# A two-block model on one core: four of six convolution filter blocks made beside the first output product, first loads reordered, and a scheduler that knows matmul kinds

## The chip, the cores and the metric

The kernel runs on one core of a Trainium2 chip. The number that counts is the device time of one launch in microseconds (us); lower is better. The core has five engines that run their own instruction streams and wait for one another by semaphores: TensorE (PE, with its weight loads shown apart as PEld), VectorE (DVE), ScalarE (ACT), GpSimd (POOL) and SyncE (SP), which here only issues DMA transfers.

## The reference

The program takes 512 tokens of width 1024 and a context of 256 tokens through a first model of two blocks, and its result through a second model of two layers with an MLP each. Everything is float32. Of the first model this matters here:

```python
for i in range(DEPTH):
    shift, scale, gate = modulation(c, w_mod[i], b_mod[i])        # silu(c) @ w_mod + b_mod
    h = rmsnorm(x, norm_g[i]) * (1 + scale) + shift
    if i == 0:                                                    # "L0"
        cshift, cscale, _ = modulation(c_ctx, w_mod[i], b_mod[i])
        hc = rmsnorm(ctx, norm_g[i]) * (1 + cscale) + cshift
        a_val, a_gate, q, k, v, b_gate = split(h @ ev_w_in)
        ck, cv = split(hc @ ev_w_in[:, k and v columns])
        # six rotary attention heads over context + tokens, a pooling mixer, gates, then
        x = x + gate * (y @ ev_w_out)                             # "L0out"
    else:                                                         # "L1"
        k = hyena_filters(...)      # from constants and small weights alone, not from x
        z = gate_o * (fft_long_conv(z, k[:, o]) + skip[o] * z)    # for o = 0, 1
        x = x + gate * (y @ od_w_out)
```

The long-convolution filters `k` are needed only in L1, but depend on nothing that comes earlier.

## The kernel before

Every product of two float32 matrices is done as three matmuls of split operands: a high part (rounded to the type fp32r) and a low part (what is left), high x high, high x low, low x high. Splitting a page costs one ScalarE activation (high) and one VectorE subtract (low). Activations, filters and tables lie in `NPG` = 52 pages of 128 x 512 floats (`pg`); weights come through a ring of three 512 KB slots (`raw`) and are split into `wh` pages. All of SyncE's transfers stand in one queue in a fixed order.

The body of the program does not run instructions; it records them into a `Plan` (from line 152 on). `Plan.schedule` then plays all engines against a model of costs (`model`, about line 250) and latencies, and puts each engine's instructions in an order: a candidate's priority is when its result is due on TensorE, shifted by `bias[phase]`, with windows `wins[(pool, phase)]` that bound how far ahead a phase may take pages or PSUM banks. `emit` (line 558) then issues all of them, which is why every row of the profile has line L558. Work that has no place of its own in the program text, such as an attention head, is a generator in the list `chains`, and `step()`, called between two gemm pieces, lets it record its next piece; `drain_chains()` (line 1589) records what is left.

The phases at the program's head, in the order in which they are recorded, and with the names that later rows use:

1. Phase "": constants, the vectors `vec` (biases, norms and the conditioning vectors), x into `xT`, the context into four pages `cT`.
2. `filt0`: two small layers that give the hidden values `hst` of the filter network.
3. `m0` (line 1232): the modulation of block 0. The activated conditioning vectors `cc` (two columns: token and context) are multiplied with `w0`, 1024 x 2048 in 16 slots of 512 KB, each with two unsplit float32 matmuls of 512 columns; small transposes against `ident` bring the rows back to columns, and a VectorE copy writes them (`m`, twice 128 x 16). From them come the scales `sc` and shifts `sh`.
4. `filt` (lines 1280 to 1352): six filter blocks, three column blocks `cb` by two orders `o`. A block loads its part of `hy_w3`, makes four 128 x 512 pages `h` by matmuls, multiplies by a decay table, sums absolute values into `acc` (the norm `hyn`), splits `h`, multiplies by the split transform matrices `cst_filt`, forms the even and odd parts `ke`, `ko`, and writes them to the DRAM tensor `kf`. The pieces are recorded by `filters()`.
5. `L0norm` (line 1369): norm sums and the scaled, shifted and split activations of context and x (`SCALAR_TENSOR_TENSOR` with `sc`, then with `sh`), the rotary table `rope` in four pages.
6. `L0kv`, `L0q`, `L0 gemm 0..2`, heads 0 to 5, then `L0out` (line 1600), the L1 norm and the L1 products, in which the hyena chains read `kf`.

A further background, phase `mods`, sums the modulation weights of all later layers with 128 VectorE instructions of their own (`mraw`).

## Time and profile before

| | |
|---|---|
| median of 3 runs | 1899.92 us (1899.1 to 1905.7) |
| the profiled execution's own time | 1898.62 us |
| its span in the trace | 1896.8 us |
| TensorE busy | 1834.3 us, 97% of the span |
| VectorE busy | 1542.9 us, 81% |
| ScalarE busy | 1026.6 us, 54% |
| GpSimd busy | 196.8 us, 10% |
| mean granted TensorE clock | 0.982 |

The own time is 1.8 us longer than the span, and the median lies 1.3 us above the own time. "Busy" counts the time in which an engine executes; TensorE's includes matmuls that run slower than they could. The granted clock is the share of full TensorE speed that the chip gave.

### The profile page before, as it was taken

The page shows a single profiled execution, that of the slowest core. Times are in us where ns is not written, and L with a number is a line of the kernel's source. Part 1 is how long each engine was busy: PE and PEld are TensorE (multiplying, and loading weights), DVE is VectorE, ACT ScalarE, POOL GpSimd, SP SyncE. Part 2 cuts the span into 40 slices and gives each one's busy share as a digit, 9 for nine tenths or more (in the row PEclk, how much of TensorE's full clock was granted, in tenths as well). Part 3 has the DMA queues.
Part 4 walks back from the last instruction along what each step waited for, and adds up shares of the span by engine and source line. Part 5 has one row for each costly group of instructions (what it writes and reads, how often), then busy time and mean ns, then how long its engine had stood idle before and what let it go on. Part 6 is the DMA issues. An engine that isn't in the chain of part 4 may idle for free.

```text
span 1896.8 us, 33344 instructions
## 1 busy us (share of the span) xinstructions
PE 1834.3 (97%) x12451; PEld 1645.8 (87%) x12451; DVE 1542.9 (81%) x3419; ACT 1026.6 (54%) x2112; POOL 196.8 (10%) x206
## 2 busy tenths in 40 slices
PE   7999999999999999999999999989999999999997
PEld 2789887988888988868888899988877889999997
DVE  6877898789986799677999877698966899776677
ACT  5666666453334565654664445574754457444455
POOL 0230010001110010021200000032101220000000
PEclk9899999999999999999999999999999989999999
DMA  8743543355432356311247422334541124323321
GB/s 281 221 132 103 193 154 112 122 194 177 137 133 78 119 169 210 96 45 45 90 161 240 155 100 89 102 108 167 184 145 45 46 78 140 106 90 101 100 90 68
DMA packets 88244, 243.19 MB, mean 128 GB/s; under 512 B 10060, under 2 KB 27248, under 8 KB 87825
## 3 DMA queue, kind: packets, MB, share of 16 engines
q1 hardware_dynamic: 88080, 241.05, 38.7%
q8 instruction: 98, 1.61, 0.3%
q14 instruction: 66, 0.53, 0.1%
HBM read 232.63 MB, written 8.39 MB: 127 GB/s over the span
## 4 chain that ended last, share of the span: by engine, by line
PE 83%; DVE 12%; ACT 2%; issue 2%; DMA 1%; POOL 0%; SPq 0%; DVEq 0%; ACTq 0%
PE ps L558 83%; DVE pg L558 7%; DVE sa L558 2%; ACT pg L558 2%; DVE wh L558 1%; DVE mraw L558 1%; ACT wh L558 0%; DMA raw<-in_w_dram 0%; DVE w L558 0%; POOL xT L558 0%; DMA vec<-in_vec_dram 0%; DVE xT L558 0%; SPq L558 0%; DVE sb L558 0%; ACT L558 0%
## 5 line engine op out<-in xcount | busy, mean ns | idle before, releaser
L558 PE MATMUL ps<-pg,wh 128*128 128x256 f32 (+1 forms) x6336 | 1101.6, 329 | 4.2 <-ACT pg L558 3.8
L558 PEld LDWEIGHTS ps<-pg,wh 128*128 128x128 f32 x6336 | 921.0, 190 | 107.5 <-ACT pg L558 5.7
L558 PE MATMUL ps<-wh,pg 128*128 128x256 f32 (+2 forms) x2976 | 379.6, 283 | 5.3 <-ACT pg L558 4.7
L558 ACT ACTIVATE wh<-raw 128x1024 fp32r<-128x1024 f32 (+3 forms) x280 | 257.8, 924 | 226.6 <-PE ps L558 222.6
L558 PEld LDWEIGHTS ps<-wh,pg 128*128 128x128 f32 x2976 | 364.3, 189 | 9.8 <-ACT pg L558 6.1
L558 DVE TENSOR_TENSOR pg<-pg 128x256 f32<-128x256 f32 (+4 forms) x656 | 317.5, 516 | 45.4 <-ACT pg L558 35.7
L558 DVE TENSOR_TENSOR wh<-raw,wh 128x1024 fp32r<-128x1024 f32 (+3 forms) x280 | 295.4, 1060 | 69.0 <-ACT wh L558 52.7
L558 ACT ACTIVATE pg<-pg 128x256 f32<-128x256 f32 (+5 forms) x630 | 274.0, 472 | 143.3 <-DVE pg L558 81.1
L558 PE MATMUL ps<-pg 128*128 128x256 f32 (+9 forms) x1776 | 264.6, 303 | 9.5 <-DVE pg L558 3.6
L558 PEld LDWEIGHTS ps<-pg 128*128 128x128 f32 (+5 forms) x1776 | 225.6, 188 | 43.5 <-issue 16.5
L558 DVE TENSOR_TENSOR pg<-pg,ps 128x256 f32<-128x256 f32 (+1 forms) x392 | 174.8, 465 | 59.6 <-PE ps L558 55.7
L558 POOL TENSOR_TENSOR pg<-pg 128x512 f32<-128x512 f32 (+4 forms) x101 | 120.7, 1202 | 858.0 <-ACT pg L558 434.6
L558 DVE TENSOR_TENSOR pg<-ps,pg 128x512 fp32r<-128x512 f32 (+8 forms) x278 | 146.4, 561 | 42.1 <-ACT pg L558 27.3
L558 DVE CUSTOM_DVE_ANT_0 mraw<-mraw,crow 128x1024 f32<-128x1024 f32 x128 | 155.4, 1220 | 8.5 <-DMA mraw<-in_wmT_dram 5.5
L558 ACT ACTIVATE pg<-ps 128x512 fp32r<-128x512 f32 (+4 forms) x212 | 105.0, 523 | 100.1 <-PE ps L558 80.0
L558 ACT COPY pg<-ps 128x256 f32<-128x256 f32 (+4 forms) x192 | 82.7, 445 | 106.2 <-PE ps L558 87.5
L558 ACT ACTIVATE wh<-w 128x512 fp32r<-128x512 f32 x112 | 70.1, 629 | 124.1 <-PE ps L558 104.4
L558 DVE TENSOR_TENSOR wh<-w,wh 128x512 fp32r<-128x512 f32 x112 | 76.7, 686 | 29.1 <-PE ps L558 17.2
L558 PE MATMUL ps<-ident,pg 128*128 128x128 f32 (+1 forms) x513 | 83.9, 279 | 5.0 <-DVE pg L558 3.8
L558 PEld LDWEIGHTS ps<-ident,pg 128*128 128x128 f32 (+1 forms) x513 | 63.3, 144 | 16.2 <-ACT pg L558 4.2
L558 ACT ACTIVATE pg<-ps,sa 128x512 f32<-128x512 f32 (+3 forms) x112 | 60.5, 550 | 29.6 <-DVE sa L558 19.1
L558 DVE TENSOR_REDUCE sa<-ps 128x1 f32<-128x512 f32 (+4 forms) x96 | 51.2, 571 | 11.4 <-PE ps L558 11.1
(139 smaller groups left out, 1095.4 us busy)
## 6 DMA issues: line engine op xcount, KB each, us to landing
mraw<-in_wmT_dram SPq DMA_DIRECT2D x128, 512.0 KB, 4.3
raw<-in_w_up_dram SPq DMA_DIRECT2D x64, 512.0 KB, 3.3
raw<-in_w_down_dram SPq DMA_DIRECT2D x64, 512.0 KB, 3.3
raw<-in_w_in_dram SPq DMA_DIRECT2D x32, 512.0 KB, 4.1
raw<-in_od_w_in_dram SPq DMA_DIRECT2D x28, 512.0 KB, 3.6
raw<-in_ev_w_in_dram SPq DMA_DIRECT2D x20, 512.0 KB, 3.7
raw<-in_w_dram SPq DMA_DIRECT2D x16, 512.0 KB, 4.1
raw<-in_w_o_dram SPq DMA_DIRECT2D x16, 512.0 KB, 3.3
```

The source lines that it names most:

```text
L558: o.fn(*[r(v) for v in o.args], **{k: r(v) for k, v in o.kw.items()})
```

## The change

1. `NF = 2`: only the first two filter blocks are recorded in the start (`filt`). The other four become a chain `filt 1`, appended after `drain_chains()` and stepped by the pieces of L0out and, through a new `step()` in `cross()`, by those that lead from L0out over the L1 norm into the first L1 product. The chain loads and splits the transform matrices a second time; for the split pages three of the four pairs lie in the weight pool `w4`.
2. A block's work is recorded in two parities, with a yield after each page. The odd part `ko` is a VectorE subtract from PSUM (before: a ScalarE copy and a GpSimd subtract), the norm is finished block by block, the decay table is loaded per block and parity.
3. `w0` comes in 32 loads of 256 KB into `pg` pages instead of 16 of 512 KB into the `raw` ring. The loads of x, context and `vec` are phases of their own, with biases of their own for SyncE (`("SP", "m0"): -30`).
4. The rotary table is stored once per head pair and broadcast: 0.5 MB instead of 1 MB, two pages instead of four, twice as many VectorE products of half the size.
5. The scheduler's model charges TensorE for a change between four kinds of matmul (`TURN`: fp32r, transpose, float32, small float32), prefers to stay in a kind (`stick`), and many biases and windows have other values.

The program has 12,059 TensorE matmuls before and after. VectorE has 3453 instructions instead of 3419, ScalarE 1911 instead of 1919, GpSimd 204 instead of 206, SyncE 588 transfers instead of 564.

```diff
--- before.py
+++ after.py
-FL = (0,)
...
-KO = (1,1,)
+NF = 2
...
-    fill=0.5, ahead=3.0, near=0.0,
+    fill=0.5, ahead=2.0, near=0.0, stick=10,
...
-        "": -15, "L0 gemm 0": -8, "L0 gemm 2": -8, "L0norm": 20, "L0out": -215, "L0q": 106, "L1 gemm 0": 145,
...
+        "": -15, ("SP", "L1out"): 8, ("SP", "m0"): -30, "L0 gemm 0": -8, "L0 gemm 2": -8, "L0norm": 20,
+        "L0out": -15, "L0q": 106, "L1 gemm 0": 265, "L1 gemm 1": 22, "L1f": 68, "L1norm": 270, "L1out": -7,
...
+    TURN = ((0.0, 0.0, 0.085, 0.185), (0.0, 0.0, 0.09, 0.12), (0.085, 0.0, 0.0, 0.1), (0.3, 0.2, 0.21, 0.0))
+    stick = 10.0
...
+                op.kind = 0 if f else 3 if a[1].shape[0] <= 64 or w in (31, 64) else 2
...
+                    if s <= ms + self.near:
+                        v = o.bl + (self.stick if e == "PE" and o.kind == kind > 1 else 0.0)
+                        if v > bb:
+                            b, bb, bs = o, v, s
...
+                s, kind = max(s, tfree[e] + self.TURN[kind][o.kind]), o.kind
...
             pl.ph = ph
             for f in fs:
                 f()
+                step()
...
+    pl.ph = "x"
     for k in range(0, KT, 4):
         D_(xall[:, k:k + 4], a["xT"][:, k:k + 4])
     cT = [pg(name="cT") for _ in range(KT // 2)]
+    pl.ph = "ctx"
     for k in range(KT // 2):
         D_(cT[k], a["ctxT"][:, k])
+    pl.ph = "vec"
...
     for j in range(2):
         pa = [mmt(), mmt()]
         for k in range(KT):
-            raw = wraw()[:, :D]
-            D_(raw, a["w0"][j, k])
             for hh in range(2):
-                T.matmul(pa[hh][0:2], cc[:, k, :], raw[:, hh * S:(hh + 1) * S], start=(k == 0), stop=(k == KT - 1))
-        row = w4()
+                raw = pg()
+                D_(raw, a["w0"][j, k, :, hh * S:(hh + 1) * S])
+                T.matmul(pa[hh][0:2], cc[:, k, :], raw, start=(k == 0), stop=(k == KT - 1))
+        row = [pg(), pg()]
         for hh in range(2):
...
-    def hyena_filters(hst):
+    def hyena_filters(hst, todo):
         fm = []
         for i in range(4):
             fr = pg()
             D_(fr, a["cst_filt"][:, i * S:(i + 1) * S])
-            fm.append(split(fr))
+            t = [pl.alloc("w4", S).bitcast(F32R) for _ in range(2)] if i < 3 else [None, None]
+            fm.append(split(fr, hi=t[0], lo=t[1]))
         yield
-        for cb in range(3):
-            dec = [pg(), pg()]
-            for i in range(2):
-                D_(dec[i].rearrange("p (t n) -> p t n", t=2),
-                                  a["cst_decay"].rearrange("p (t n) -> p t n", t=4)[:, 2 * i:2 * i + 2, cb * 256:cb * 256 + 256])
-            for o in range(2):
...
-                acc = None
+        for cb, o in todo:
+            w3 = pg()
...
+            acc, xs = None, []
+            for par in range(2):
+                dec = pg()
+                D_(dec.rearrange("p (t n) -> p t n", t=2),
+                   a["cst_decay"].rearrange("p (t n) -> p t n", t=4)[:, 2 * par:2 * par + 2, cb * 256:cb * 256 + 256])
                 ab = []
-                for jt in range(4):
+                for jt in (2 * par, 2 * par + 1):
                     ps = axt()
                     js = slice(jt * P, jt * P + P)
                     for d_ in range(2):
...
                     h = pg()
-                    dj = dec[jt // 2][:, (jt % 2) * 256:(jt % 2) * 256 + 256]
+                    dj = dec[:, (jt % 2) * 256:(jt % 2) * 256 + 256]
                     V.tensor_mul(h.rearrange("p (d n) -> p d n", d=2), ps.rearrange("p (d n) -> p d n", d=2),
                                  dj.unsqueeze(1).to_broadcast([P, 2, 256]))
                     hb, ha = pg(), hp()
...
                         V.tensor_copy(h[0:1, 256:], h[0:1, :256])
                     else:
                         G.tensor_tensor(acc, acc, ha, op=OP.add)
-                    ab.append(split(h, eng=V if jt in FL else G))
-                ps = axt()
-                for i in range(2):
-                    T.matmul(ps[:, i:i + 1], acc[:, i * P:(i + 1) * P], ones[:, 0:1], start=True, stop=True)
-                V.tensor_copy(hyn[:, o, 2 * cb:2 * cb + 2], ps[:, :2])
+                    ab.append(split(h))
+                    yield
+                if par:
+                    ps = axt()
+                    for i in range(2):
+                        T.matmul(ps[:, i:i + 1], acc[:, i * P:(i + 1) * P], ones[:, 0:1], start=True, stop=True)
+                    hy = hyn[:, o, 2 * cb:2 * cb + 2]
+                    V.tensor_scalar(hy, ps[:, :2], 1e-6, 1024.0, op0=OP.add, op1=OP.mult)
+                    V.reciprocal(hy, hy)
                 for ft in range(2):
...
-                    xs, ke, ko = pg(), pg(), pg()
-                    A.copy(xs, px)
-                    V.tensor_add(ke, xs, py)
-                    if KO[ft]:
-                        ys = pg()
-                        A.copy(ys, py)
-                        G.tensor_tensor(ko, xs, ys, op=OP.subtract)
-                    else:
-                        V.tensor_sub(ko, xs, py)
+                    ps = axt()
+                    for rs in range(2):
+                        fh, fl = fm[2 * par + rs]
+                        cs = slice(rs * 256, rs * 256 + 256)
+                        for i in range(2):
+                            fs = slice(i * 256 + ft * P, i * 256 + ft * P + P)
+                            xh, xl = ab[i]
+                            mm3(ps[:, cs], (fh[:, fs], fl[:, fs]), (xh[:, cs], xl[:, cs]), i == 0, i == 1)
+                    if not par:
+                        xs.append(pg())
+                        A.copy(xs[ft], ps)
+                        continue
+                    ke, ko = pg(), pg()
+                    V.tensor_add(ke, xs[ft], ps)
+                    V.tensor_sub(ko, xs[ft], ps)
...
                 yield
-        V.tensor_scalar(hyn.rearrange("p a b -> p (a b)"), hyn.rearrange("p a b -> p (a b)"), 1e-6, 1024.0,
-                        op0=OP.add, op1=OP.mult)
-        V.reciprocal(hyn.rearrange("p a b -> p (a b)"), hyn.rearrange("p a b -> p (a b)"))
-        yield
-
...
-    filters(9)
+
+    todo = [(cb, o) for cb in range(3) for o in range(2)]
+    for _ in hyena_filters(hst, todo[:NF]):
+        pass
...
-    rope = [pg(name="rope") for _ in range(4)]
-    for i in range(4):
+    rope = [pg(name="rope") for _ in range(2)]
+    for i in range(2):
...
     q_block(0)
-    filters()
...
     drain_chains()
+    chains.append(("filt 1", hyena_filters(hst, todo[NF:])))
```

The table of numbers acts through the order of the instructions. Three places show it; every instruction of the kernel is issued at one line, L558 before and L564 after.

SyncE, the queue's head (`in_w` is w0, `in_hy_w` the filter network's weights, `in_cst_filt` the transform matrices). Before:

```order
L558 DMA pg<-in_cst_emb_dram 33x512
L558 DMA pg<-in_hy_w_dram 33x64
L558 DMA raw_368<-in_w_dram 128x1024
L558 DMA raw_369<-in_w_dram 128x1024
L558 DMA pg<-in_hy_w_dram 64x64 x2
L558 DMA raw_370<-in_w_dram 128x1024
L558 DMA vec_366<-in_vec_dram 128x83
L558 DMA pg<-in_hy_w_dram 64x2x256 x2
L558 DMA pg<-in_cst_decay_dram 128x2x256 x2
L558 DMA ident<-in_cst_ident_dram 128x128
L558 DMA pg<-in_cst_filt_dram 128x512 x4
L558 DMA pg<-in_hy_w_dram 64x2x256 x4
```

After:

```order
L564 DMA pg<-in_cst_emb_dram 33x512
L564 DMA pg<-in_hy_w_dram 33x64
L564 DMA vec_366<-in_vec_dram 128x83
L564 DMA pg<-in_hy_w_dram 64x64 x2
L564 DMA pg<-in_hy_w_dram 64x2x256 x2
L564 DMA pg<-in_cst_decay_dram 128x2x256
L564 DMA pg<-in_cst_filt_dram 128x512
L564 DMA ident<-in_cst_ident_dram 128x128
L564 DMA pg<-in_cst_filt_dram 128x512
L564 DMA pg<-in_w_dram 128x512 x2
L564 DMA pg<-in_ctxT_dram 128x512
L564 DMA pg<-in_cst_decay_dram 128x2x256
```

The `vec` load moves from eighth to third transfer and the context comes early; the first piece of w0 moves from third to twelfth place, after filter weights, a decay table and two transform matrices. The last piece of w0 stands behind 16.54 MB in the new queue, behind 15.75 MB in the old.

VectorE, from the second modulation copy `m_397` on. Before:

```order
L558 COPY m_397<-ps 128x16
L558 TENSOR_TENSOR pg<-pg,ps 128x512
L558 TENSOR_TENSOR pg<-pg 128x256 x3
L558 TENSOR_TENSOR pg<-pg 128x512
L558 TENSOR_TENSOR pg<-pg 128x256 x7
L558 TENSOR_TENSOR pg<-ps,pg 128x512 x2
L558 COPY hyn<-ps 128x2
L558 TENSOR_TENSOR pg<-ps,pg 128x512
L558 TENSOR_TENSOR pg<-pg,ps 128x512
L558 TENSOR_TENSOR pg<-ps,pg 128x512
L558 TENSOR_TENSOR pg<-pg 128x256 x2
```

After:

```order
L564 COPY m_397<-ps 128x16
L564 TENSOR_TENSOR wh_376<-raw_370,wh_375 128x1024
L564 TENSOR_TENSOR sc_399<-m_397,vec_366 128x8 x2
L564 SCALAR_TENSOR_TENSOR sc_399<-sc_399,vec_366 128x8 x2
L564 SCALAR_TENSOR_TENSOR pg<-pg,sc_399,ps 128x256 x4
L564 SCALAR_TENSOR_TENSOR pg<-pg,sh_398 128x256
L564 SCALAR_TENSOR_TENSOR pg<-xT,sc_399,ps 128x512
```

Before, filter pages (`pg<-ps,pg`, `pg<-pg`, `hyn`) follow the copy, and `sc` comes 24 rows after the last of these; after, `sc` and the first scaled activations (`xT` is the token input) follow almost at once, and no filter instruction stands between.

TensorE, in L0out from the last block of 17 matmuls of head 5 on (`wh` are split weights of L0out, `w_2940`, `w_2953`, `w_3002` transform matrices). Before:

```order
L558 MATMUL ps<-pg 128x256 x17
L558 MATMUL ps<-pg,wh_375 128x512
L558 MATMUL ps<-pg,wh_376 128x512
L558 MATMUL ps<-pg,wh_375 128x512 x2
L558 MATMUL ps<-pg,wh_376 128x512
L558 MATMUL ps<-pg,wh_375 128x512 x2
L558 MATMUL ps<-pg,wh_376 128x512
L558 MATMUL ps<-pg,wh_373 128x512 x2
```

After:

```order
L564 MATMUL ps<-pg 128x256 x17
L564 MATMUL ps<-pg,wh_371 128x512 x2
L564 MATMUL ps<-pg,wh_372 128x512
L564 MATMUL ps<-pg,w_2940 128x256
L564 MATMUL ps<-pg,wh_373 128x512
L564 MATMUL ps<-pg,w_2940 128x256
L564 MATMUL ps<-pg,w_2953 128x256
L564 MATMUL ps<-pg,wh_373 128x512
L564 MATMUL ps<-pg,w_2940 128x256 x2
L564 MATMUL ps<-pg,wh_374 128x512
L564 MATMUL ps<-pg,w_2953 128x256
L564 MATMUL ps<-pg,w_2940 128x256
```

Before, L0out's matmuls stand in runs of their own; after, matmuls of 256 columns of the moved filter blocks lie between them one by one. The same 256 filter matmuls that stood ahead of or among the first projections now lie in heads 4 and 5, L0out, the L1 norm and the first two L1 products. From about matmul 9210 of 12,059 to the end the orders of TensorE are the same, also from 5432 to 7427.

## Rows read from the trace of the kernel before

**Rows 1.** the page, its span and section 1 (busy us, share of span, instructions).
```profile
span 1896.8 us, 33344 instructions
PE 1834.3 (97%) x12451; PEld 1645.8 (87%) x12451; DVE 1542.9 (81%) x3419; ACT 1026.6 (54%) x2112; POOL 196.8 (10%) x206
```

**Rows 2.** the chain that ended last: by engine, then one long piece.
```profile
PE 83%; DVE 12%; ACT 2%; issue 2%; DMA 1%; POOL 0%; SPq 0%; DVEq 0%; ACTq 0%
...
117.99 117.18 PE ps L558 x808
```

**Rows 3.** windows: engines' busy us (instructions), granted PE clock, DMA share, GB/s.
```profile
0.00:20.00 20.00, 9.64 (x20) 1.62 (x20) 9.35 (x22) 5.76 (x11) 1.56 (x10) 1.00 0.89 271
20.00:60.00 40.00, 39.15 (x166) 17.79 (x167) 31.75 (x72) 24.03 (x48) 2.72 (x3) 0.96 0.78 266
60.00:100.00 40.00, 34.55 (x240) 31.46 (x241) 36.36 (x86) 28.20 (x55) 16.64 (x14) 0.87 0.78 230
100.00:120.00 20.00, 17.32 (x143) 16.91 (x143) 19.75 (x44) 16.69 (x38) 9.34 (x8) 1.00 0.24 68
120.00:235.00 115.00, 115.00 (x795) 105.73 (x794) 89.30 (x215) 68.64 (x159) 1.72 (x2) 1.00 0.45 147
235.00:330.00 95.00, 89.59 (x538) 76.98 (x537) 84.43 (x200) 60.11 (x140) 4.83 (x3) 0.96 0.43 139
330.00:600.00 270.00, 270.00 (x1712) 243.02 (x1711) 227.80 (x424) 108.54 (x173) 29.41 (x23) 1.00 0.44 148
```

**Rows 4.** PE's timeline to 137.6 us: start, length, form, count, idle before.
```profile
9.27 6.14 PE L558 MATMUL ps<-raw,cc 128*2 128x512 f32 x8 [5.21 <-ACT cc L558]
32.18 1.88 PE L558 MATMUL ps<-raw,cc 128*2 128x512 f32 x4
67.19 0.41 PE L558 MATMUL ps<-ident,w 2*128 2x2 f32 x4
98.23 1.76 PE L558 MATMUL ps<-wh,pg 128*128 128x256 f32 x13
117.99 1.70 PE L558 MATMUL ps<-pg 128*128 128x256 f32 x12 [2.49 <-DVE pg L558]
...
119.53 18.07 PE L558 MATMUL ps<-wh,pg 128*128 128x256 f32 x152
```

**Rows 5.** DVE's timeline from the second modulation copy on.
```profile
67.91 0.16 DVE L558 COPY m<-ps 128x16 f32<-128x16 f32 x1
...
87.28 0.16 DVE L558 TENSOR_TENSOR sc<-m,vec 128x8 f32<-128x8 f32 x1
...
90.22 2.43 DVE L558 SCALAR_TENSOR_TENSOR pg<-pg,sc,ps 128x256 f32<-128x256 f32 x6
...
112.59 5.35 DVE L558 SCALAR_TENSOR_TENSOR pg<-xT,sc,ps 128x512 f32<-128x512 f32 x8
```

**Rows 6.** VectorE's groups by form: count, busy us, mean ns, idle before and releasers.
```profile
L558 DVE TENSOR_TENSOR pg<-pg 128x256 f32<-128x256 f32 x250 | 100.5, 428 | 12.6 <-ACT pg L558 9.7 <-DMA pg<-in_hy_w_dram 1.6 <-POOL pg L558 0.6
L558 DVE TENSOR_TENSOR pg<-pg 128x512 fp32r<-128x512 f32 x116 | 77.8, 688 | 11.9 <-ACT pg L558 6.5 <-PE ps L558 4.8
L558 DVE TENSOR_TENSOR pg<-pg,ps 128x512 f32<-128x512 f32 x76 | 50.9, 680 | 14.8 <-PE ps L558 14.3 <-ACT pg L558 0.2
L558 DVE TENSOR_TENSOR pg<-ps,pg 128x512 f32<-128x512 f32 x78 | 50.3, 680 | 9.7 <-PE ps L558 9.4
```

**Rows 7.** windows again: the first loads, then heads and first output product.
```profile
5.00:30.00 25.00, 17.67 (x46) 4.62 (x47) 14.85 (x33) 8.45 (x19) 0.87 (x1) 0.93 1.02 317
30.00:65.00 35.00, 35.00 (x168) 17.83 (x167) 28.91 (x65) 22.41 (x45) 2.72 (x3) 1.00 0.69 239
380.00:460.00 80.00, 80.00 (x470) 70.22 (x469) 74.17 (x129) 34.19 (x49) 7.05 (x5) 1.00 0.56 192
460.00:520.00 60.00, 60.00 (x385) 54.16 (x384) 58.57 (x120) 19.33 (x30) 10.29 (x8) 1.00 0.42 139
```

**Rows 8.** what SyncE's DMA queue waited for, 0 to 120 us: total, times, longest.
```profile
SPq L558 <- PE ps L558: 28.6, 15, 4.4
```

More of the change, by code (lines that the diff above doesn't have):

```diff
@@ L137 @@
     __slots__ = ("eng", "fn", "args", "kw", "deps", "succ", "cost", "bufs", "idx", "bl", "npred", "est", "tab",
-                 "bytes", "cols", "start", "fin", "due", "ph", "ret", "ss", "se", "port", "other", "est2")
+                 "bytes", "cols", "start", "fin", "due", "ph", "ret", "ss", "se", "port", "other", "est2", "kind")
 class Eng:
@@ L257, in model @@
             if m == "transpose":
-                op.cost, op.cols = 0.109, 256 * a[1].shape[0] / P
+                op.cost, op.cols, op.kind = 0.109, 256 * a[1].shape[0] / P, 1
             else:
@@ L474, in schedule @@
                 for s, o in cand:
-                    if s <= ms + self.near and o.bl > bb:
-                        b, bb, bs = o, o.bl, s
+                    if s <= ms + self.near:
+                        v = o.bl + (self.stick if e == "PE" and o.kind == kind > 1 else 0.0)
+                        if v > bb:
+                            b, bb, bs = o, v, s
                 if bs < ps:
@@ L778, in tile_two_blocks @@
         D_(t, a[n])
+    pl.ph = ""
     def vcol(name):
@@ L1352, in hyena_filters @@
                 yield
-        V.tensor_scalar(hyn.rearrange("p a b -> p (a b)"), hyn.rearrange("p a b -> p (a b)"), 1e-6, 1024.0,
-                        op0=OP.add, op1=OP.mult)
-        V.reciprocal(hyn.rearrange("p a b -> p (a b)"), hyn.rearrange("p a b -> p (a b)"))
-        yield
-    filt = hyena_filters(hst)
-    def filters(n=99):
-        old, pl.ph = pl.ph, "filt"
-        for _ in range(n):
-            if next(filt, filt) is filt:
-                break
-        pl.ph = old
-    filters(9)
+    todo = [(cb, o) for cb in range(3) for o in range(2)]
+    for _ in hyena_filters(hst, todo[:NF]):
+        pass
     pl.ph = "L0norm"
@@ L1399, in ropeit @@
             t1, t2 = pg(), pg()
[L1400 to L1405 removed]
+            for tt in range(2):
+                ts = slice(tt * 256, tt * 256 + 256)
+                rs = slice((2 * tp + tt) * P, (2 * tp + tt) * P + P)
+                G.tensor_tensor(t1[:, ts].rearrange("p (h f) -> p h f", h=2), q[:, ts].rearrange("p (h f) -> p h f", h=2),
+                                rope[0][:, rs].unsqueeze(1).to_broadcast([P, 2, P]), op=OP.mult)
+                qv = q[:, ts].rearrange("p (h a s f) -> p h a s f", h=2, s=2, f=32)
+                sv = rope[1][:, rs].rearrange("p (a s f) -> p a s f", s=2, f=32)
+                tv = t2[:, ts].rearrange("p (h a s f) -> p h a s f", h=2, s=2, f=32)
+                for s in range(2):
+                    V.tensor_mul(tv[:, :, :, s], qv[:, :, :, 1 - s], sv[:, :, s].unsqueeze(1).to_broadcast([P, 2, 2, 32]))
             V.tensor_add(q, t1, t2)
```

53 lines of the change are left out of this document (18 added, 35 removed), and 32 rows, old and new, of the table wins.

## The prediction

> **What bounds the kernel now.** I began with the page's first section. TensorE is busy for 97% of a span of 1896.8 us, VectorE for 81% [rows 1]: nothing but TensorE's work and the holes in it sets the time. The chain of waits says the same, 83% TensorE and 12% VectorE, and its piece from 117.99 to 235.17 us has no hole [rows 2]. Since the matmuls stay the same in number and form, the change can only win holes, stretches at a lower clock and turns between kinds of matmul, or make new ones.
>
> So I next looked at windows, to find the holes [rows 3]. TensorE idles 10.36 us in the first 20, 0.85 in 20 to 60, 5.45 in 60 to 100 and 2.68 in 100 to 120: 19.3 us in 120. From 120 to 235 it is never idle, from 330 to 600 never either. Its clock is granted at 0.96 in 20 to 60 and at 0.87 in 60 to 100. If only the levels 1.2 and 2.4 GHz alternate, a mean of 0.87 is 40 x 0.13 = 5.2 us lost, and 0.96 another 1.6: 6.8 us.
>
> The same loss from the other side, by counting work. Of the matmuls that run until 119.53 us there are 6 filter blocks of 64 matmuls of 256 columns; 152 of that shape take 18.07 us [rows 4], 0.119 each, so a block is 7.6 us and six are 45.7. The modulation is 64 records at 1.88 / 4 = 0.47 us, 30.1 us. The timeline shows 48 first projections (`ps<-wh,pg`, from 98.23 on, 13 in the first run) before 119.53: 5.7 us. Small transposes, sums and the filter's hidden layers I put at 6.5 us, an estimate from rows like the 0.41 us for four of them [rows 4]. The sum is 88 us; the start loses 119.5 - 88 = 31.5 us. That is the stake of this change.
>
> Why it loses them is in two timelines. TensorE waits 5.21 us for the conditioning vectors before its first modulation matmul, at 9.27, and eight records there take 6.14 us, 0.77 each against 0.47 later [rows 4]. And VectorE: the second modulation copy is done at 68.07, but `sc` comes at 87.28, the first scaled context page at 90.22 and the token pages from 112.59 [rows 5]. VectorE is busy 36.36 of 40 us in 60 to 100, and 19.75 of 20 in 100 to 120 [rows 3]; it works through filter pages in that gap, as its order shows. TensorE has only filter blocks to do meanwhile, and they wait for that same VectorE.
>
> **Part 1: the start.** Two blocks stay, four go. What has to be done up to the second modulation copy is then, on TensorE, 30.1 + 2 x 7.6 + 4 = 49.3 us; begun at about 9 us it would end at 58, if fed. On VectorE, the 86 rows that the new order puts ahead of that copy, at the durations of their forms (0.43 us for 256 columns, 0.68 to 0.69 for 512 [rows 6]), come to about 47 us; begun at about 5 and with some 7 us of waits they end at 59. On the queue, 16.54 MB stand up to the last piece of w0. From 5 to 30 us the present queue, a mix of loads of 64 to 512 KB, moves 317 GB/s with its engines at a share of 1.02 [rows 7]; at that rate the last piece lands at 2 + 52 = 54. From 30 to 65 it moved 239 GB/s at 0.69, but it was not always the limit: in the first 120 us it waited 28.6 us in 15 pieces for a buffer that TensorE still read [rows 8]. The loads now go to 52 pages instead of a ring of three. So three things end between 54 and 59, and I take 59 for the copy, with 54 and 66 as bounds.
>
> From there `sc` follows at once. The activations are eight context pages, each a scale and a shift, and eight token pages. The scales take 2.43 / 6 = 0.41 and 5.35 / 8 = 0.67 us [rows 5], and with shifts and low parts at 0.43 and 0.69 [rows 6] VectorE needs some 17 to 18 us for what is on it. TensorE has 42 filter matmuls left (5.0 us) and each context page releases 12 projections, 96 in all, 11.4 us, before token pages are needed. Feeding it costs about 3 us, an estimate. TensorE therefore has done 49.3 us of work at 59 + 3 = 62, a loss of 12.7; the feeding and the clock add 3 to 4. The loss is 16 to 17 instead of 31.5: a gain of 15. A copy at 54 gives 20, at 66 gives 8.
>
> A rule of the Trainium skill speaks against the split of w0. The page SBUF — State Buffer, section "The DMA setup-cost knee", gives 224 GB/s for a transfer of 256 KiB and wants transfers combined into larger ones. By it the 16.54 MB would need 74 us, the copy would come at 76 and nothing would be gained (the first rival, at its far end). The trace does not agree: 317 GB/s were moved with most loads at 512 KB or less [rows 7], as several are in flight together.
>
> **Part 2: where the four blocks go.** TensorE's work is the same, 30.5 us, only later: between heads 4 and 5 and the first L1 products, in the trace of before about 330 to 460 us. TensorE is busy all of that, at full clock [rows 3, 7], so the 30.5 us appear there in full and are already counted, since the start got shorter by work and holes. What counts is VectorE. A block costs it four products, four absolute values, four sums, four low parts and four even and odd parts: 4 x (0.68 + 0.43 + 0.43 + 0.69) + 4 x 0.68 = 11.6 us [rows 6]. The odd parts were GpSimd's before. Four blocks and the second split of the transform matrices (4 x 0.69) are 49 us. From 330 to 600 VectorE has 227.8 us of 270 [rows 3]; with them 277 of 301, 92%. It fits as a whole, but not everywhere: 380 to 460 is 74.17 of 80 and 460 to 520 is 58.57 of 60 [rows 7]. And heads 4 and 5 now have hardly any L0out to fill them, which the order shows: by sums of the forms TensorE has 26.6 us in that stretch and VectorE 31.4. That is 5 us at most; some of it is covered. I take 4 us for the part, with 0 and 10 as bounds.
>
> **Part 3: the rest.** The second load of the matrices (1 MB) and of decay tables goes through a queue at a share of 0.44 [rows 3], with pages free well ahead: nothing. The rotary products, 32 of half the size for 16, add about 32 x 0.43 - 16 x 0.68 = 3 us to VectorE after 120, where it has 89.30 of 115 [rows 3] and TensorE is fed: nothing; if that cover failed, 3. The holes and the clock in 235 to 330 (5.4 us idle, 0.96) belong to heads that are not moved: unchanged. Reordered pieces in 600 to 880 and 1200 to 1530 have both signs: 0, within 4 either way. The last 2850 matmuls keep their order, so the end keeps its time.
>
> **Sum.** -15 + 4 = -11 on the profiled execution's 1898.62 us: 1887.6, and I say **1887**. The median of the runs lies 1.3 us above that execution, which is inside my error.
>
> **Rivals.**
> First, the wait only changes its name. The start is then bound by loads: at the 239 GB/s of 30 to 65 us [rows 7] 16.54 MB take 69 us, the copy comes at 71, TensorE idles for want of w0, which now stands behind filter tables, and 3 us of the 15 are left. With the 4 us behind it the time is about 1899, no change. For it: w0 moved back in the queue. Against it: the rate of the first 25 us, and a queue that waited for buffers. (The page's curve named above would put the copy 5 us later still, at 76, and the time at 1904.) A change that does not reach the hardware, its modelled turns being wrong, ends at the same place.
>
> Second, slower: VectorE becomes the bound in 330 to 520. If the scheduler packs the four blocks into the 140 us from 380 to 520, VectorE has 132.7 + 49 = 182 us of work at some 97% possible use, 187, where TensorE has 140 + 30.5 = 170.5: 17 us of holes, and TensorE loses perhaps 8 more in its clock, as the 0.87 beside 5.45 us of idle in 60 to 100 shows [rows 3]. That is 25 us against 15, or 13 where the start wins less: 1909 to 1911. It decides from the point at which the new holes pass 15 us. For it: 98% in 460 to 520. Against it: the blocks are spread from head 4 to the first L1 products, and half of those stretches has room.
>
> Third, a larger gain. If grouping by kinds and the even load of VectorE also take the holes of 235 to 330, 5.4 us and 3.8 of clock, and part 2 costs nothing, the time is 1898.6 - 15 - 9 = 1875.
>
> **How the numbers follow.** Forecast 0.52, the first rival 0.17, the second 0.13, the third 0.18. The forecast's own range is 1879 to 1895 (gains of 20 and 8, costs of 0 to 5). A measurement tells 0.5% or 9.5 us from no change: below 1890.4 or above 1909.4. Of the forecast's share 0.40 is faster and 0.12 the same; the third rival is faster; the first is the same; the second is slower by more than 9.5 us in 0.10 and the same in 0.03. Faster 0.58, same 0.32, slower 0.10. The range for 8 in 10 runs from 1873 to 1903: it holds the forecast, the first and most of the third.
>
> **What would show it.** In the profile of the changed kernel the second modulation copy should end near 59 us and the first scaled context page some 2 us later, TensorE's idle time in the first 100 us should be 12 to 15 us, and unbroken projections should begin near 75 instead of 119.5. Part 1 is wrong if the copy comes after 66 or TensorE names w0 as what it waited for. Part 2 is right if TensorE stays above 97% around L0out, and wrong if its idle time there, with VectorE as the releaser, passes 10 us. The forecast as a whole is wrong if the start has its gain and the total does not show it, or the other way round.

## The result, and the profile after

| | before | changed |
|---|---|---|
| median, 4 runs each | 1901.96 us (1899.1 to 1905.7) | 1881.05 us (1880.39 to 1885.21) |
| the profiled execution's own time | 1898.62 us | 1881.66 us |
| mean granted TensorE clock | 0.982 | 0.991 |

The ratio of the changed kernel to the one before is 0.9894, with a 95% interval of 0.9869 to 0.9918. The forecast was 1887 us in a range of 1873 to 1903. The number came out within 6 us; the way to it did not, as the next tables show.

The page of the changed kernel, its span and first section, to set beside [rows 1]:

```profile
span 1879.8 us, 33476 instructions
PE 1815.2 (97%) x12451; PEld 1630.2 (87%) x12451; DVE 1548.7 (82%) x3453; ACT 1017.0 (54%) x2100; POOL 194.4 (10%) x204
```

TensorE is busy 19 us less in a span 17 us shorter, with the same matmuls: it did the same work with less waste inside its busy time. VectorE has 6 us more.

Windows of the changed kernel (columns as in [rows 3]):

```profile
0.00:20.00 20.00, 8.12 (x16) 1.15 (x16) 8.37 (x21) 6.50 (x15) 1.48 (x6) 1.00 0.66 210
20.00:60.00 40.00, 32.95 (x138) 15.87 (x139) 30.48 (x82) 22.02 (x41) 0.72 (x1) 0.91 0.80 261
60.00:100.00 40.00, 40.00 (x282) 31.89 (x281) 27.13 (x60) 25.23 (x64) 5.48 (x10) 1.00 0.64 200
100.00:120.00 20.00, 20.00 (x175) 19.96 (x174) 19.10 (x69) 8.40 (x30) 0.00 (x0) 1.00 0.22 68
235.00:330.00 95.00, 90.86 (x594) 81.11 (x593) 84.79 (x197) 58.39 (x123) 6.44 (x9) 1.00 0.39 125
330.00:600.00 270.00, 268.04 (x1728) 242.00 (x1727) 243.57 (x464) 111.37 (x178) 37.61 (x30) 1.00 0.46 156
```

TensorE is never idle from 60 to 120 us, where it idled 8.1 us before; it idles 11.9 and 7.1 us in the first two windows instead of 10.4 and 0.9. From 235 to 330 its clock is no longer lowered. From 330 to 600 VectorE has 243.57 instead of 227.80 us, and TensorE idles 2 us.

The same start in two pieces, kernel before, then changed kernel:

```profile
0.00:70.00 70.00, 58.79 (x256) 27.43 (x257) 48.11 (x106) 36.74 (x71) 5.59 (x14) 0.98 0.80 259
70.00:120.00 50.00, 41.86 (x312) 40.35 (x311) 49.11 (x116) 37.95 (x79) 24.68 (x20) 0.90 0.58 170
```

```profile
0.00:70.00 70.00, 51.07 (x189) 20.52 (x189) 41.42 (x106) 28.53 (x55) 2.20 (x7) 0.95 0.76 244
70.00:120.00 50.00, 50.00 (x419) 48.35 (x418) 43.65 (x124) 33.64 (x94) 5.48 (x10) 1.00 0.44 138
```

By 120 us TensorE has been busy for 100.65 and 101.07 us. The holes only changed their place: 11.2 and 8.1 us before and after 70 us became 18.9 and none.

To compare stages of all kernels, I use two measures from the traces. The first is the **time at equal work**. TensorE has 12,451 records in every trace, and in all fourteen traces the first 3700 of them are the same by form, only in another order; so are the first 5410, 8540 and 9620. In the kernel before these points are reached at 615.8, 887.7, 1362.6 and 1554.2 us, and the moved blocks are done by the first. The time between two points holds the same matmuls in every kernel and needs no price. The second is the **loss**, for the start, where kernels differ in their blocks: the time that has passed, less the price of the matmuls begun so far, where a record is priced at the median step, over the traces of before and changed, between two records of its form that follow one another (0.118 us for 256 columns at full clock). Holes, lowered clock and turns between kinds all count in it. The expectations below quote losses from an earlier set of prices, by which the start lost 38.8 us before and 37.9 in the changed kernel, and the stretch from 1400 to 1560 us 27.6 and 14.5; by the prices here these are 35.3 and 30.6, 21.4 and 10.8.

| us | loss, 0 to 120 us | to record 3700 | 3700 to 5410 | 5410 to 8540 | 8540 to 9620 | 9620 to the last | median | ratio to before, interval |
|---|---|---|---|---|---|---|---|---|
| before | 35.3 | 615.8 | 271.9 | 475.0 | 191.6 | 332.5 | 1901.96 |  |
| before, second profile | 36.7 | 619.2 | 271.2 | 475.6 | 190.5 | 332.2 | 1900.65 (one run) |  |
| changed | 30.6 | 611.6 | 268.8 | 476.4 | 180.3 | 332.6 | 1881.05 | 0.9894 (0.9869 to 0.9918) |
| changed, second profile | 30.0 | 610.4 | 270.1 | 477.2 | 183.4 | 332.4 | 1885.48 (one run) |  |
| all_six_first | 55.6 | 633.6 | 269.0 | 478.6 | 181.0 | 332.6 | 1910.52 | 1.0058 (1.0039 to 1.0077) |
| four_first | 40.5 | 620.7 | 274.3 | 477.9 | 183.3 | 334.7 | 1902.62 | 1.0005 (0.9985 to 1.0024) |
| three_first | 29.7 | 612.1 | 268.6 | 477.7 | 183.0 | 332.4 | 1885.55 | 0.9926 (0.9903 to 0.9949) |
| new_table_old_work | 45.7 | 624.0 | 270.6 | 480.1 | 183.4 | 332.1 | 1904.54 | 1.0033 (1.0014 to 1.0052) |
| kinds_alone | 43.0 | 624.8 | 271.5 | 476.5 | 177.7 | 332.6 | 1896.67 | 0.9978 (0.9958 to 0.9999) |
| old_table | 33.5 | 629.7 | 271.5 | 475.9 | 199.4 | 332.4 | 1909.03 | 1.0049 (1.0027 to 1.0072) |
| no_kinds | 34.2 | 625.1 | 273.3 | 477.6 | 193.5 | 332.1 | 1909.85 | 1.0044 (1.0025 to 1.0063) |
| w0_sooner_10 | 26.8 | 610.1 | 269.2 | 479.1 | 180.7 | 334.9 | 1886.37 | 0.9923 (0.9902 to 0.9945) |
| w0_sooner_20 | 26.1 | 608.1 | 270.1 | 478.1 | 183.4 | 335.0 | 1883.88 | 0.9912 (0.9889 to 0.9936) |
| w0_sooner_24 | 36.1 | 618.4 | 271.6 | 475.6 | 182.9 | 332.4 | 1888.88 | 0.9945 (0.9924 to 0.9965) |

Two profiles of one kernel differ by up to 3.4 us in a stretch, so less than that is not read here. The traced execution is not always near the median: it took 1920.73 us for old_table, 1913.61 for no_kinds, 1892.77 for w0_sooner_24 and 1906.49 for all_six_first.

The changed kernel is 4.2 us ahead at record 3700, 7.3 at 5410, 5.8 at 8540, 17.1 at 9620 and 17.0 at the last record. The second profiles of both give 8.8, 9.9, 8.3, 15.4 and 15.1; numbers in brackets below are this second pair. Within the first 3700 records two more points can be compared. At 164.8 us the kernel before has begun 935 records; the changed kernel has begun the same ones, less those of four blocks, at 128.2 us. The blocks' 256 matmuls and 16 sums are priced at 32.0 us, so the lead is 4.6 us (7.7). At 294.9 us the kernel before has begun 1698, and the changed one the same but for the four blocks at 253.4 us, just ahead of the first matmuls of these blocks: a lead of 9.6 us (14.2).

### The profile page after: what moved, and what is told of

Read it like the earlier page. It is cut to its first block, busy times and chain, and to the rows that moved or that the text cites. A ratio compares the mean times of both kernels' runs of the same rounds, so it can differ in the third digit from the quotient of the medians.

```text
span 1879.8 us, 33476 instructions
## 1 busy us (share of the span) xinstructions
PE 1815.2 (97%) x12451; PEld 1630.2 (87%) x12451; DVE 1548.7 (82%) x3453; ACT 1017.0 (54%) x2100; POOL 194.4 (10%) x204
## 5 line engine op out<-in xcount | busy, mean ns | idle before, releaser
L564 PE MATMUL ps<-pg,wh 128*128 128x256 f32 (+1 forms) x6336 | 1108.3, 328 | 7.4 <-ACT pg L564 4.7
L564 PEld LDWEIGHTS ps<-pg,wh 128*128 128x128 f32 x6336 | 919.1, 189 | 108.6 <-ACT pg L564 7.0
L564 PE MATMUL ps<-wh,pg 128*128 128x256 f32 (+2 forms) x2976 | 378.8, 283 | 5.0 <-ACT pg L564 5.0
L564 ACT ACTIVATE wh<-raw 128x1024 fp32r<-128x1024 f32 (+3 forms) x280 | 257.7, 923 | 231.6 <-PE ps L564 223.7
L564 PEld LDWEIGHTS ps<-wh,pg 128*128 128x128 f32 x2976 | 364.5, 189 | 8.8 <-ACT pg L564 6.1
L564 DVE TENSOR_TENSOR wh<-raw,wh 128x1024 fp32r<-128x1024 f32 (+3 forms) x280 | 297.7, 1066 | 66.7 <-ACT wh L564 51.5
L564 DVE TENSOR_TENSOR pg<-pg 128x256 f32<-128x256 f32 (+4 forms) x671 | 317.3, 508 | 37.6 <-ACT pg L564 33.3
L564 ACT ACTIVATE pg<-pg 128x256 f32<-128x256 f32 (+4 forms) x628 | 274.4, 472 | 128.3 <-DVE pg L564 75.0
L564 PE MATMUL ps<-pg 128*128 128x256 f32 (+7 forms) x1560 | 235.6, 300 | 7.5 <-DMA pg<-in_hy_w_dram 2.9
L564 DVE TENSOR_TENSOR pg<-pg,ps 128x256 f32<-128x256 f32 (+1 forms) x404 | 182.9, 473 | 59.7 <-PE ps L564 55.9
L564 PEld LDWEIGHTS ps<-pg 128*128 128x128 f32 (+4 forms) x1560 | 199.8, 184 | 33.8 <-issue 7.9
L564 POOL TENSOR_TENSOR pg<-pg 128x512 f32<-128x512 f32 (+4 forms) x96 | 114.7, 1199 | 908.9 <-ACT pg L564 488.0
L564 ACT ACTIVATE pg<-ps 128x512 fp32r<-128x512 f32 (+4 forms) x212 | 104.9, 524 | 116.2 <-PE ps L564 91.5
L564 DVE TENSOR_TENSOR pg<-ps,pg 128x512 f32<-128x512 f32 (+8 forms) x278 | 146.1, 561 | 26.1 <-ACT pg L564 20.6
L564 DVE CUSTOM_DVE_ANT_0 mraw<-mraw,crow 128x1024 f32<-128x1024 f32 x128 | 155.8, 1222 | 11.2 <-DMA mraw<-in_wmT_dram 11.2
L564 ACT ACTIVATE wh<-w 128x512 fp32r<-128x512 f32 x112 | 70.3, 630 | 127.3 <-PE ps L564 103.0
L564 ACT COPY pg<-ps 128x256 f32<-128x256 f32 (+5 forms) x184 | 78.3, 438 | 99.6 <-PE ps L564 96.9
L564 DVE TENSOR_TENSOR wh<-w,wh 128x512 fp32r<-128x512 f32 x112 | 77.0, 688 | 31.7 <-PE ps L564 19.5
L564 PE MATMUL ps<-ident,pg 128*128 128x128 f32 (+1 forms) x529 | 82.8, 276 | 5.0 <-ACT pg L564 1.8
L564 PEld LDWEIGHTS ps<-ident,pg 128*128 128x128 f32 (+1 forms) x529 | 63.1, 143 | 17.7 <-ACT pg L564 5.9
L564 ACT ACTIVATE pg<-ps,sa 128x512 f32<-128x512 f32 (+3 forms) x112 | 60.6, 553 | 28.8 <-DVE sa L564 27.0
L564 PE MATMUL ps<-pg,w 128*128 128x256 f32 (+1 forms) x408 | 68.0, 284 | 1.4 <-DVE pg L564 1.4
```

The source lines that it names most:

```text
L564: o.fn(*[r(v) for v in o.args], **{k: r(v) for k, v in o.kw.items()})
```

## The experiments

**Is it chance?** Both kernels once more, unchanged, for a second trace.

> The kernel before, unchanged, profiled a second time, to see whether the stretches at the lower clock stand where they stood (79, 260, 851, 912, 929, 1267, 1445 and 1537 us, 68 us in all). Theory A, the late gain is the clock's and the clock falls by chance: the stretches move, and their sum differs by more than 15 us. Theory B, the clock follows the order of the work: the same stretches return within a few us, those at 1445 and 1537 among them.

> The changed kernel, unchanged, profiled a second time (34 us at the lower clock in the first profile, none between 1469 and 1875). Theory A, chance: a stretch appears near 1540 us in this one, or the sum passes 50 us. Theory B, the order sets it: the sum stays at 30 to 45 us and 1530 to 1570 stays at full clock.

The mean granted clock was 0.983 and 0.990, against 0.982 and 0.991; the clock's records in the traces have 68 and 68 us at the lower level before, and 34 and 41 in the changed kernel. The stretches of the table agree within 3.4 us. Most of the named stretches at the lower clock return within 6 us of their place, 1450 and 1539 us among them; that at 929 does not, and each kernel has two that are new. From record 8540 to 9620 the two profiles of before take 191.6 and 190.5 us, those of the changed kernel 180.3 and 183.4. So the late gain belongs to the program: theory B of both, in the main.

**All six blocks in the start again.**

```diff
-NF = 2
+NF = 6
...
-    chains.append(("filt 1", hyena_filters(hst, todo[NF:])))
+    if todo[NF:]:
+        chains.append(("filt 1", hyena_filters(hst, todo[NF:])))
```

> The changed kernel with all six filter blocks in the start again and no filter chain at L0out; loads, rotary table and scheduler stay as changed. Theory A, the start pays as predicted: about 15 us of the gain go, less the 4 that the blocks cost later, so 1891 to 1896 us. Theory B, the start is bound by its loads and the gain is made after 800 us: within 4 us of the changed kernel, 1877 to 1885 us.

1910.52 us, worse than both theories. Both fall: the start is not indifferent to the blocks, as B had it, and the blocks cost more there than the 15 us of A. VectorE's timeline of this kernel, second modulation copy, first `sc`, last scaled token pages:

```profile
64.18 0.17 DVE L564 COPY m<-ps 128x16 f32<-128x16 f32 x1
...
90.54 0.17 DVE L564 TENSOR_TENSOR sc<-m,vec 128x8 f32<-128x8 f32 x1
...
113.58 1.39 DVE L564 SCALAR_TENSOR_TENSOR pg<-xT,sc,ps 128x512 f32<-128x512 f32 x2
```

The copy comes sooner than in either kernel, and then 26 us pass until `sc`: filter pages stand between, as they did before [rows 5], only longer. TensorE from 60 to 120 us, here and in the changed kernel:

```profile
60.00:120.00 60.00, 39.68 (x258) 37.08 (x256) 58.23 (x135) 44.13 (x82) 13.60 (x14) 0.80 0.66 202
```

```profile
60.00:120.00 60.00, 60.00 (x454) 51.85 (x453) 46.22 (x128) 33.64 (x94) 5.48 (x10) 1.00 0.50 156
```

Moving the four blocks gives 25 us by 120 us (loss 55.6 and 30.6), by the mechanism that was forecast, if everything else is as in the changed kernel; at record 3700, with the blocks done in both, 22.0 us of it are left.

**The scheduler's part alone**, on the work and loads of before (the whole scheduler part of the diff on the old program).

> The kernel before with the whole scheduler part of the change and nothing else (kinds, stick, costs, windows, biases; work and loads as before). Theory A, the moved blocks make the gain: 1896 to 1902 us. Theory B, the order of the late phases makes it: 1882 to 1889 us, with TensorE's loss after 800 us 12 to 15 us below that of the kernel before.

1904.54 us, a miss for both theories in the time. The late gain is there, but smaller than B had it: 183.4 us from record 8540 to 9620 instead of 191.6, 8 us and not 12 to 15. What B misses is the start, which loses 45.7 us instead of 35.3.

**The moved work alone**, with the scheduler of before (its `SCHED`, `TURN` all zero, no stick).

> All of the changed work (two blocks in the start, four in the chain, w0 in 32 loads, small rotary table) with the scheduler of before: its windows and biases, no kinds. Theory C, the moved blocks win in the start and the new table wins after 800 us, each by itself: w0 stands early in this queue, so the start should lose 22 to 28 us by 120 us instead of 38, and the stretch from 800 to 1560 as much as before (87 to 93 us): 1884 to 1892 us. Theory D, the two need each other, as the six blocks under the new table were slower than before: 1897 to 1905 us.

1909.03 us, beyond the range of theory D and on its side: the two need each other. Here w0 stands first in the queue and the second copy is done at 44.4 us, the soonest of all; the filter work was put off instead. The copy, then the window from 60 to 80 us of this kernel:

```profile
44.21 0.16 DVE L564 COPY m<-ps 128x16 f32<-128x16 f32 x1
```

```profile
60.00:80.00 20.00, 13.61 (x77) 12.96 (x77) 20.00 (x55) 16.02 (x29) 7.82 (x11) 0.67 0.73 239
```

VectorE is full, TensorE idles 6.4 us at a clock of 0.67, and the first scaled page starts at 68.36, 24 us after the copy. The wait after the copy has come back with a third of the blocks. The traced execution is one of three of ten that took 1920 us; the other seven took 1907 to 1910, and no trace shows whether the wait is as long in those.

**The kinds taken out.**

```diff
-    TURN = ((0.0, 0.0, 0.085, 0.185), (0.0, 0.0, 0.09, 0.12), (0.085, 0.0, 0.0, 0.1), (0.3, 0.2, 0.21, 0.0))
-    stick = 10.0
+    TURN = ((0.0,) * 4,) * 4
+    stick = 0.0
...
-    fill=0.5, ahead=2.0, near=0.0, stick=10,
+    fill=0.5, ahead=2.0, near=0.0, stick=0,
```

> The changed kernel without the kinds in the scheduler's model: TURN all zero, no stick; windows and biases as changed. Theory K, the kinds make the gain after 800 us by laying alike matmuls together: most of the 12 us between 800 and 1560 us go, 1890 to 1896 us. Theory L, the late biases and windows make it: 1879 to 1886 us.

Theory K for the late stretch, and more than it priced: record 8540 to 9620 takes 193.5 us, as long as before (191.6, 190.5), and the first 3700 records take 13.5 us longer than in the changed kernel.

**The kinds put in alone**, in the kernel before (`TURN`, `stick`, the small term in the matmul cost; nothing else).

> The kernel before with the kinds alone: TURN, stick and the small term in the matmul cost; work, loads, windows and biases as before. Kinds have been in every kernel so far that loses only 14 to 19 us from 1400 to 1560 us, and were absent in the three that lose 28 to 31. Theory K: the kinds make this gain by themselves, 14 to 20 us lost there, 1886 to 1892 us if the start stays as before. Theory M: it needs the new biases too, 25 us or more lost there, 1896 to 1904 us.

177.7 us from record 8540 to 9620, where the kernel before takes 191.6: theory K for that stretch. The time is 1896.67 and not below 1892, since the first 3700 records, with six blocks in the start, take 9.0 us longer. In the table every kernel with kinds takes 177.7 to 183.4 us for the late stretch, every one without 190.5 to 199.4. The window around it, in the order before, kinds alone, changed, changed without kinds:

```profile
1400.00:1560.00 160.00, 153.89 (x946) 130.66 (x945) 124.27 (x313) 81.58 (x158) 32.98 (x37) 0.95 0.18 60
```

```profile
1400.00:1560.00 160.00, 156.29 (x1018) 134.57 (x1017) 130.50 (x333) 89.23 (x174) 29.65 (x32) 0.99 0.19 64
```

```profile
1400.00:1560.00 160.00, 154.87 (x1053) 136.19 (x1052) 136.23 (x339) 92.97 (x181) 29.74 (x33) 0.99 0.20 70
```

```profile
1400.00:1560.00 160.00, 155.63 (x879) 128.89 (x878) 118.95 (x289) 82.49 (x159) 27.59 (x26) 0.92 0.20 64
```

Of these four, those with kinds have a clock of 0.99 there, those without 0.95 and 0.92. What the order did is seen at the 32 narrow matmuls of the gated linear attention. TensorE's timeline of before (one piece), then the same matmuls with the kinds alone:

```profile
1442.09 0.48 PE L558 MATMUL ps<-pg 32*128 32x128 f32 x2
1442.51 0.33 PE L558 MATMUL ps<-pg,w 128*128 128x128 f32 x1
1442.77 0.48 PE L558 MATMUL ps<-pg 32*128 32x128 f32 x2
1443.18 0.33 PE L558 MATMUL ps<-causalr,identr 128*128 128x128 f32 x1
1443.43 0.48 PE L558 MATMUL ps<-pg 32*128 32x128 f32 x2
```

```profile
1451.80 1.26 PE L565 MATMUL ps<-pg 32*128 32x128 f32 x16
```

Each pair stood alone between others; now 16 run in a row. In the groups by form of 1400 to 1560 us, before and changed (count, busy us, mean ns of one):

```profile
L558 PE MATMUL ps<-pg 128*64 128x128 f32 x32 | 6.3, 307 | 0.0
L558 PE MATMUL ps<-pg 32*128 32x128 f32 x32 | 5.9, 354 | 0.0
```

```profile
L564 PE MATMUL ps<-pg 128*64 128x128 f32 x32 | 3.3, 292 | 0.0
...
L564 PE MATMUL ps<-pg 32*128 32x128 f32 x32 | 2.7, 286 | 0.0
```

The same 64 matmuls kept TensorE busy for 12.2 us before and 6.0 after. The end of a record that stands alone overlaps the next one; counted from start to next start they took 10.6 and 5.5 us (9.7 and 5.5), and ten of the 64 records of before lie in a stretch at the lower clock. Near 1535 us a hole also matters; windows of before, then of the changed kernel, which does the same work here some 15 us sooner:

```profile
1530.00:1540.00 10.00, 6.20 (x46) 5.75 (x44) 9.53 (x24) 7.22 (x16) 4.81 (x7) 0.84 0.00 0
1540.00:1550.00 10.00, 10.00 (x59) 10.00 (x60) 8.65 (x35) 0.00 (x0) 2.12 (x4) 0.65 0.75 262
```

```profile
1510.00:1520.00 10.00, 9.87 (x85) 9.80 (x83) 9.81 (x28) 8.22 (x17) 6.49 (x9) 1.00 0.33 107
1520.00:1530.00 10.00, 9.25 (x71) 8.36 (x70) 10.00 (x30) 4.29 (x10) 1.20 (x2) 1.00 0.14 45
1530.00:1540.00 10.00, 8.27 (x69) 7.90 (x68) 9.26 (x36) 3.93 (x9) 5.96 (x9) 1.00 0.46 166
```

Before, TensorE idles 3.8 us and then runs ten microseconds at 0.65; in the changed kernel it idles 0.1, 0.8 and 1.7 us and the clock stays. How much of the late gain is clock can be read from two traces that have the same 13.7 us at the lower clock between records 8540 and 9620: the second profile of before takes 190.5 us, w0_sooner_20, with kinds, 183.4. So about 7 us are not the clock. In the first profiles the time at the lower clock also fell, from 17.1 to 3.4 us, which at half speed is 6.8 us at most. What the kinds' two parts, `TURN` and `stick`, give each was not tried.

**How many blocks?** Three and four in the start (`NF = 3`, `NF = 4`).

> The changed kernel with three filter blocks in the start and three in the chain. Theory G: the start waits for bytes, w0, context and x, and filter blocks are the only work of TensorE that needs few of them; a third block fills holes, the wall time of the start stays and 7.6 us of work leave the stretch after 330 us: 1873 to 1878 us. Theory A: each block in the start costs what it holds up: 5 to 8 us more than the changed kernel, 1886 to 1890 us.

> The same with four blocks in the start and two in the chain. Theory G: still holes enough, but VectorE begins to hold up the activations: 1872 to 1882 us. Theory A: 10 to 15 us more than the changed kernel, 1891 to 1897 us.

Neither theory has both. With three the start loses 29.7 us, with four 40.5, with six 55.6, with two 30.6. So the third block still fits into holes, and no gain is left of it in the time (1885.55 us, ratio 0.9926); with four the blocks hold up the activations, and TensorE waits 8.6 us for VectorE's pages between 60 and 120 us.

**w0 sooner in the queue**, as the second copy cannot come before its last pieces: the bias `("SP", "m0")` at -10, -20 and -24 instead of -30.

> The changed kernel with the bias of SyncE's w0 loads at -10 instead of -30: 16 of the 32 pieces stand right behind the hidden layers' weights, ahead of filter tables and context. Theory E, the start waits for w0, which stands too late in the queue: the second modulation copy moves from 73 to 58 to 64 us, the start loses 28 to 32 us instead of 38 by 120 us, 1872 to 1878 us in all. Rival F, the filter blocks and the context then come as much later as w0 comes sooner: the copy moves, the projections begin within 3 us of 78 us, 1879 to 1884 us.

> The same at -20: six pieces of w0 ahead of the filter tables. Theory E: half of the step, copy at 64 to 69 us, 1876 to 1880 us. Rival F: no change, 1879 to 1884 us.

> The changed kernel with the w0 bias at -24: 14 of the 32 pieces stand ahead of the last filter table instead of 6, and from its matmul 1690 of 12,059 on TensorE's order is that of the changed kernel, which was not so at -10 and -20. Theory E, w0 stands too late and what the start wins is kept where the late order stays: second modulation copy at 64 to 69 us, 33 to 36 us lost by 120 us instead of 38, the late stretches lose the same, 1876 to 1879 us. Rival H: what the start wins is given back later whatever the order, 1881 to 1885 us.

The second modulation copy in VectorE's timeline, for -10, -20 and -24:

```profile
63.09 0.17 DVE L564 COPY m<-ps 128x16 f32<-128x16 f32 x1
```

```profile
67.22 0.17 DVE L564 COPY m<-ps 128x16 f32<-128x16 f32 x1 [2.07 <-PE ps L564]
```

```profile
76.56 0.17 DVE L564 COPY m<-ps 128x16 f32<-128x16 f32 x1 [6.74 <-PE ps L564]
```

At -10 and -20 the copy came 10 and 6 us sooner and the start lost 4 us less (26.8 and 26.1 instead of 30.6), part of theory E. The times are not below the changed kernel's, and the intervals of the ratios overlap: from record 3700 to the last these kernels took 1264.0 and 1266.5 us, the changed kernel 1258.1 (1263.1). The third run was to keep the late order and so the gain, and missed: the copy came 3 us later than at -30, and the start lost 36.1. The place in the queue alone doesn't set when w0 is there. From record 3700 on that kernel took 1262.5 us, between the two profiles of the changed one, so rival H isn't supported either. No version beat the changed kernel.

## Why the prediction was right in its number and wrong in its way

**The copy at 59 us: wrong.** It came at 73.46. VectorE's timeline of the changed kernel, to set beside [rows 5]: copy, `sc`, first scaled context pages, last scaled token pages.

```profile
73.29 0.17 DVE L564 COPY m<-ps 128x16 f32<-128x16 f32 x1 [8.65 <-PE ps L564]
...
74.54 0.24 DVE L564 TENSOR_TENSOR sc<-m,vec 128x8 f32<-128x8 f32 x2
...
74.94 1.66 DVE L564 SCALAR_TENSOR_TENSOR pg<-pg,sc,ps 128x256 f32<-128x256 f32 x4
...
84.80 1.40 DVE L564 SCALAR_TENSOR_TENSOR pg<-xT,sc,ps 128x512 f32<-128x512 f32 x2
```

TensorE's timeline, to set beside [rows 4]: the first modulation matmuls and the first unbroken projections.

```profile
12.63 3.57 PE L564 MATMUL ps<-pg,cc 128*2 128x512 f32 x4 [8.57 <-ACT w L564]
...
77.69 29.69 PE L564 MATMUL ps<-wh,pg 128*128 128x256 f32 x253
```

Unbroken projections began at 77.69; the forecast was 75, but with a copy 14 us sooner. By the prediction's own test (a copy after 66, TensorE waiting for w0) part 1 is wrong. The step that failed is "three things end between 54 and 59". TensorE was to begin its modulation matmuls at about 9 us and to be fed. It began them at 12.63 and idled 18.9 us by 60 us, 4.6 of them for w0; the profile puts the longest wait down to a ScalarE split. From 42.35 us on it had no hole, so the time lost lies ahead of that, not right ahead of the copy. Its two longest waits, total, times, longest:

```profile
PE ps L564 <- ACT w L564: 8.6, 1, 8.6
PE ps L564 <- DMA pg<-in_w_dram: 4.6, 4, 2.0
```

The queue was taken as limited by its rate, 317 GB/s. It moved 210 GB/s from 0 to 20 us and 261 from 20 to 60. SyncE's waits from 20 to 75 us, and the issue of the last eight pieces of w0:

```profile
SPq L564 <- PE ps L564: 14.8, 13, 3.8
SPq L564 <- DVE pg L564: 9.1, 5, 2.7
```

```profile
58.45 7.33 SPq L564 DMA_DIRECT2D pg<-in_w_dram  x8
```

23.9 of 55 us went into waits for pages that TensorE and VectorE still held. The prediction had seen such waits and expected the 52 pages to end them; from 0 to 75 us they only fell from 37.0 to 29.3 us. The last piece was issued at about 65 us; the copy followed 8 us later. How much of the delay the waits make is not shown, since the DMA engines were also busy at a share of 0.80 from 20 to 60 us. By the curve in the Trainium skill (SBUF — State Buffer, section "The DMA setup-cost knee") the prediction had estimated a copy at 76. The curve has 224 GB/s for a transfer of 256 KiB; the trace does not agree, with 261 GB/s from 20 to 60 us, when most loads had that size and the queue stood waiting in between. The time is near, the cause is another. The first rival, with a copy at 71 and 3 us left of the 15, was nearer to this start than the forecast.

**The wait after the copy: right.** From copy to `sc` 1.1 us instead of 19, no filter page between, VectorE's activations done in some 14 us, and no idle time of TensorE. The two-block kernel against all six shows its worth, 25 us. But the loss up to 70 us rose from 21.6 to 29.8 us, and from 70 to 120 it fell from 13.6 to 0.8. The forecast priced the second and overlooked that the four blocks were work for TensorE while loads were late: taken away, they leave holes ahead of the copy (with three and four blocks in the start the loss up to 70 us is 25.9 and 24.0). So the term of -15 for the start measured -4.6 (-7.7).

**The four blocks at L0out: right, in size and place.** +4 forecast, with 0 and 10 as bounds. From the last point ahead of the blocks to record 3700 the lead fell from 9.6 (14.2) us to 4.2 (8.8), so they cost 5.4 (5.4) with all else that lies there; against six blocks, 3.0. From 330 to 600 VectorE has 16 us more and GpSimd 8, not 49, since all other work runs some 40 us sooner and part of it had left this window. In the 301 us up to 600, the stretch that the forecast had in mind, VectorE was busy for 265.5 us where it had 277. There was no stretch of holes.

**"Unchanged" heads, and "reordered pieces: 0, within 4": wrong, and here is most of the gain.** From record 8540 to 9620, which is 1362.6 to 1554.2 us before, the changed kernel took 11.3 us less (7.1). From 164.8 to 294.9 us, the first heads, the lead grew by 5.0 us (6.5), with the clock at 1.00 instead of 0.96 from 235 to 330. Record 3700 to 5410 gave 3.1 (1.1), within the 4, and 5410 to 8540 nothing. I had read the order from row 9210 on as unchanged, and the rows ahead of it as too like to matter, and gave the matmul kinds no price, though the trace of before shows one: narrow matmuls that stand alone. The third rival had the kinds, but put their gain at 235 to 330 us; 5 us were won there, but not by the kinds. That the kinds make the late gain is shown from both sides (177.7 us with them alone, 193.5 without them). The gain in the heads comes with the scheduler's windows and biases, as far as one profile each shows: from record 705 to 2080, the same by form in these kernels (136.4 to 357.1 us before), the scheduler part alone takes 4.0 us less than the kernel before, the kinds alone 0.2 more.

The sum, start, heads, blocks, then the four stretches from record 3700 on: -4.6 - 5.0 + 5.4 - 3.1 + 1.4 - 11.3 + 0.1 = -17.1, against -17.0 in the traces; in the second pair -15.2 against -15.1. The forecast's -15 + 4 + 0 = -11 was near since two errors offset: 10 us (7) too much in the start, 18 (13) too little in what it had put at nothing. That the number fits is in so far luck: by the prediction's last sign, a total that shows its gain while the start does not, the forecast as a whole was wrong. The scheduler part and the moved blocks each made the kernel slower when tried alone (1904.54, 1909.03) and faster together: with kinds the six blocks make the first 3700 records 8 to 18 us longer than before, and moving four takes that away. Why the kinds do that to a start with six blocks was not tried.

## What to carry to other kernels

Before work is moved out of a start, ask what the busiest engine does in its place while loads arrive: work that needs few bytes may be filler, not hindrance. Look in the issue queue's waits for what holds it up, buffers as well as a rate, before dividing bytes by GB/s. And count short instructions that stand alone between others of another kind: an order that lays kinds together gave 7 to 11 us in one stretch here, about as much as the start, the heads and the moved blocks did together. To compare two orders of the same work, look for points where both have begun the same instructions: between them no price is needed.

## What the runs showed that I had not expected

Stretches at the lower clock return at nearly the same work in repeated profiles: 1.8% and 1.7% of the span's clock lost before, 0.9% and 1.0% after. Of 1896.8 us that is 34 us, of 1879.8 us 17 us, a difference as large as the whole gain; yet a comparison at equal time at the lower clock leaves about 7 us of the late gain to the order itself. Thirty-two matmuls of 32 rows by 128 columns took 5.2 us from start to next start in pairs (4.4 in the second profile, at full clock throughout) and 2.6 us laid together.
